# Start offsets of the on-chip pools in a one-layer encoder kernel: all left-hand pools moved to multiples of 512 bytes

## The chip, the cores and the metric

The kernel runs on one core of a Trainium2 chip. The metric is the device time of one launch in microseconds. Before the change three runs gave a median of 2282.25 us (2280.88 to 2286.59).

## The reference, cut to what matters

One layer on x of 1024 tokens by 1024 channels, float32. `rms` is an RMS norm, `mod` an affine map per channel whose shift, scale and gate come from a condition vector.

```python
h = x + 0.5 * g1 * rms(swiglu(mod1(rms(x)), wg1, wu1, wd1))     # 1024 -> 2816 -> 1024
h = h + g2 * rms(mixer(mod2(rms(h))))
h = h + 0.5 * g3 * rms(swiglu(mod3(rms(h)), wg2, wu2, wd2))
...
def mixer(u):
    qa, ka, va, qd, kd, vd, ga, gd = split(u @ w_in)             # 1024 -> 5120
    ya = stick_breaking_attention(qa, ka, va)                    # 8 heads of 64
    yd = rms(differential_attention(qd, kd, vd))                 # 4 heads, two softmax maps
    return (sigmoid(ga) * (ya @ w_sb) + sigmoid(gd) * (yd @ w_da)) @ w_out
```

## The kernel before, in words

**Matmuls in halves.** Every float32 operand is kept as two tiles, a rounded half H and the rest L, and a product is three matmuls into one PSUM bank: H by H, H by L, L by H. `PE.matmul(out, stationary, moving)` loads the stationary operand (128 columns) into TensorE and then streams the moving one (512 columns for most). The profile writes the moving operand first: `bank<-uH,wsH` streams `uH` past the weights `wsH`. A product is thus a stream of matmuls, each with a weight load of its own that runs beside the matmul ahead of it.

**Stages, in order of time.**
- FFN 1 up (lines 298 to 300): 11 pairs of a gate and an up matrix. Each of the 22 is a 2x2 block product done with seven block products instead of eight (Strassen's scheme in Winograd's form), each of 12 matmuls: A11 B11 and A12 B21 (`start_parts`; the moving tiles are `uH`/`uL` of the first half of the tokens, 24 matmuls), then p6, p5, p7, p3, p4 with the moving tiles T2, T1, T3, B22, T4 (60 matmuls). The stationary tiles `wsH`/`wsL` come from `wpool`. So 44 matrices over the two FFNs, 84 matmuls each.
- FFN 1 down (583 to 585): stationary `sbH`/`sbL`, moving `tbH`/`tbL`, both in pool `ffb`.
- Mixer (813 to 1087): the jobs QJob, KJob and GateJob stream `u` tiles past `wsH`/`wsL` (line 813 to 817, output `pps`), for the first half of the tokens and for the second; VJob has them the other way round (`vps`, 256 columns). They are handed out a few matmuls at a time between the attention's own work: `qk` (938, 939), the transposes (955, 956), and weights by values (1021, 1066, 1068: moving `tH`/`tL`, stationary `v`).
- Merge (200 to 202): `bps` streams second-half `u` tiles (holding the attention's results) past `wsH`/`wsL`; `ops` streams output weights past the merged tiles `mH`/`mL`. The weights `wo` come from `wpool`, but of those for the second half of the output columns (q = 1) the first two of four come from a pool of the stage itself (tag `wx`).
- FFN 2 up and down as FFN 1.

**Where tiles lie.** Each pool is a run of bytes in every SBUF partition; each tile's size is rounded up to 32 bytes. Left-hand pools stack upwards: `const`, `upool` (first-half `u` tiles), `wpool` (`wsH`, `wsL`, `raw`), `mpool` (small tiles of the norms), and above them one stage's pools after the other (`ffa`, `fft`, `fft2`, `ffb0`, `ffb`, `u1` with the second-half `u` tiles, `mixa` with `q`, `kd`, `kl`, `v`, and `mrg` with `mH`, `mL`, `wx`). Right-hand pools hang from the top: `ypool`, `late`, and during the attention `mixb` (`be`, `f`, `ex`, `tH`, `tL`). A pool's first byte is the end of the one it stands on, so the tiles of `const` set where `upool` and `wpool` begin, and those of `mpool` where all stage pools begin. Matmul operands are slices of whole multiples of 512 bytes into their tiles (128 columns of 4 bytes), so an operand's offset modulo 512 is that of its tile.

The bytes before the change: 1152 that belong to the runtime and built-in constants; then `const`, 512 + 512 + 32 + 32 + 288 + 96 + 32 + 32 and eight tiles of 32, 1792, so that `upool` begins at 2944 = 5 x 512 + 384. `upool` and `wpool` hold multiples of 512. `mpool` has 2048 + 12 x 32 = 2432, which takes the stage pools to 256 modulo 512.

Of the kernel before, what the change touches and what calls it, by code (L numbers as in the profile page):

```python
# [12 lines left out]
F32 = mybir.dt.float32  # L13
F32R = mybir.dt.float32r
BF16 = mybir.dt.bfloat16
# [5 lines left out]
P = 128  # L21
D = 1024
S = 1024
NK = D // P
# [22 lines left out]
def build(ctx, tc, A, out):  # L47
# [3 lines left out]
    const = ctx.enter_context(tc.tile_pool(name="const", bufs=1))  # L51
# [3 lines left out]
    extra = {}  # L55
    mpool = ctx.enter_context(tc.tile_pool(name="mpool", bufs=1))

    ident = const.tile([P, P], F32, name="ident")
    make_identity(nc, ident)
    ones = const.tile([P, P], F32, name="ones")  # L60
    V.memset(ones, 1.0)

    cT = const.tile([P, NK], F32, name="cT")
    SP.dma_start(cT, A["cT"])
    csil = const.tile([P, NK], F32, name="csil")
    ACT.activation(csil, cT, AF.Silu)
    badaT = const.tile([P, 72], F32, name="badaT")
    npreT = const.tile([P, 3 * NK], F32, name="npreT")
    eps = const.tile([P, 1], F32, name="eps")
    V.memset(eps, EPS)  # L70
# [73 lines left out]

    def rstd_of(src, parts=1):

        junk = mpool.tile([P, D], BF16, name="junk", tag="junk", bufs=1)
        ss = mpool.tile([P, 2], F32, name="ss", tag="ss", bufs=4)
        w = D // parts
        for n in range(parts):  # L150
            ACT.activation(junk[:, n * w:(n + 1) * w], src[:, n * w:(n + 1) * w], AF.Square, scale=1.0 / 32.0, accum_out=ss[:, n:n + 1])
        if parts == 2:
            V.tensor_add(ss[:, 0:1], ss[:, 0:1], ss[:, 1:2])
        sq = mpool.tile([P, 1], F32, name="sq", tag="sq", bufs=4)
        ACT.activation(sq, ss[:, 0:1], AF.Sqrt, bias=eps)
        r = mpool.tile([P, 1], F32, name="rs", tag="rs", bufs=4)
        V.reciprocal(r, sq)
        return r
# [7 lines left out]
    def pre_norm(src, eng=V):  # L166

        r = rstd_of(src)
        if eng is ACT:
            ACT.mul(src, src, r)  # L170
        else:
            eng.tensor_scalar_mul(src, src, r)
# [36 lines left out]
    def post_norm_tile(y, g, res, dst, parts=1, tail=False):  # L209

        r = rstd_of(y, parts)
        cuts = [slice(0, HALF), slice(HALF, D)] if tail else [slice(0, D)]
        for c in cuts:
            V.scalar_tensor_tensor(y[:, c], y[:, c], r, g[:, c], ALU.mult, ALU.mult)
        for c in cuts:
            V.tensor_add(y[:, c], y[:, c], res[:, c])
            SP.dma_start(dst[:, c], y[:, c])
# [544 lines left out]
    pending = ffn("wg1", "wu1", "wd1", start0, pending0, steps1, lambda c: 2 if c == 1 else 5 if c < 10 else 0, steps1b, 0, lambda t: A["x"][t * P:(t + 1) * P, :], lambda t: h_dram[0][t])  # L762

    pending = mixer(locals())

    ffn("wg2", "wu2", "wd2", start_half, pending, lambda fp, psum: mod_gate(fp, psum, 2, 0.5), lambda c: 2 if c > 1 else 0, no_steps, 2, lambda t: h_dram[1][t],
# [4 lines left out]
def mixer(e):  # L771
# [14 lines left out]
    with tc.tile_pool(name="mixa", bufs=1, side="left", reuse_waits="tile") as pa, \  # L786
# [200 lines left out]
        def run_av(it, mms):  # L987
            try:
                it.send(mms)
            except StopIteration:  # L990
                pass

        def y_dst(branch, k, rows, j):
            return y_d[branch, j // 2, k // 2, rows, k % 2, (j % 2) * 256:(j % 2 + 1) * 256]
# [65 lines left out]
        def da_out(h, j, it, vt, fill):  # L1060
            pav = psum.tile([P, HALF], F32, name="pav", tag="av", bufs=1)
            o = pav[:, :256]

            def mms(low, kb, w, qs, first, last):
                cs = slice((h % 2) * P, (h % 2 + 1) * P)
                last_pe[0] = PE.matmul(o[:, qs], vt[:, kb, 0, cs], w, start=first, stop=last)
                if not low:
                    PE.matmul(o[:, qs], vt[:, kb, 1, cs], w, start=False, stop=False)

            run_av(it, mms)  # L1070
            ms = mp.tile([P, 256], F32, name="ms", tag="ms", bufs=1)
            y = mp.tile([P, 256], F32, name="yda", tag="y32", bufs=2)
            ACT.activation(ms, o, AF.Square)
            ACT.copy(y, o)
            fill(1)
            pn = psum.tile([P, HALF], F32, name="pn", tag="z", bufs=3)[:, :256]
            PE.matmul(pn, n.ones, ms, start=True, stop=True)

            V.tensor_scalar(ms, pn, 1.0 / P, EPS, ALU.mult, ALU.add)
            ln = mp.tile([P, 256], F32, name="ln", tag="ln", bufs=1)  # L1080
            ACT.activation(ln, ms, AF.Ln, scale=2.0 ** -64)
            ACT.activation(ln, ln, AF.Exp, scale=-0.5, bias=n.lnb)
            V.tensor_mul(ms, ms, ln)
            V.tensor_mul(ms, ms, ln)
            V.tensor_scalar(ms, ms, -0.5, 1.5, ALU.mult, ALU.add)
            V.scalar_tensor_tensor(ln, ln, subs, ms, ALU.mult, ALU.mult)
            V.tensor_mul(y, y, ln)
            SP.dma_start(y_dst(1, h, slice(0, P), j), y)
# [25 lines left out]
        mp = stack.enter_context(tc.tile_pool(name="mixb", bufs=1, side="right", reuse_waits="tile"))  # L1114
# [3 lines left out]
        SP.dma_start(mask_sb, A["mask_sb"])  # L1118
        dist = mp.tile([P, S], F32, name="dist")
        SP.dma_start(dist, A["dist"])  # L1120
        subT = mp.tile([P, 1], F32, name="subT")
        SP.dma_start(subT, A["subT"])
        subs = mp.tile([P, 1], F32, name="subs")
        V.tensor_scalar_mul(subs, subT, 1.0 - LAMBDA_INIT)
# [23 lines left out]
        for u in range(8):  # L1148
            sb = u < 4
            if u == 4:  # L1150

                with tc.issue_after(last_act[0].ins):
                    load = ACT.add_instruction(mybir.InstLoadActFuncSet(
                        name=nc.get_next_instruction_name(), engine=ACT.engine, act_func_set_id=EXP_LN_TABLE))
# [18 lines left out]
            def fill(n):  # L1173
                seen[0] += n * wt[si]
                advance(max(0, min(total, int(total * seen[0] / points)) - done[0]))
# [8 lines left out]
            for si, (par, j) in enumerate(steps):  # L1184
                if carry is not None:
                    next(carry[0])
                if sb:
                    ws = sb_weights(u, par, j, q, k, fill)
                else:
                    ws = da_weights(u - 4, j, q, k, fill)  # L1190
                if carry is not None:
                    carry[1]()
                if si == 0 and u % 2 == 0 and u > 0:
                    vjob = VJob(u // 4, u % 4 // 2)
                    while vjob.step():
                        pass
                it = av(ws[0], ws[1], j, fill)
                if sb:
                    carry = it, lambda par=par, j=j, it=it, u=u, vt=vjob.out, fill=fill: sb_out(u, par, j, it, vt, fill)
                else:  # L1200
                    carry = it, lambda j=j, it=it, u=u, vt=vjob.out, fill=fill: da_out(u - 4, j, it, vt, fill)
# [150 lines left out]
```

## Time and profile before

| what | value |
|---|---|
| three runs, median | 2282.25 us |
| the profiled execution, first to last instruction (span) | 2278.7 us |
| the same, whole | not given apart from its span; the median is 3.55 us over the span |
| TensorE busy | 2189.4 us (96%), 10420 matmuls |
| VectorE, ScalarE, GpSimd busy | 1566.4, 1043.7, 70.0 us |
| mean granted TensorE clock | 0.989 |

In the timeline a row is one matmul: its start in us, how long it took, its engine and line, what it writes, what it streams, what is loaded. A matmul's row lasts about 0.4 us, but the next starts long before it ends, since they are pipelined. So a stream's pace is read from the starts: the time between the starts of two rows, divided by the number of matmuls between them. Below this is called the **gap**. In the groups "x352" is how many there are, and the numbers behind the bar are busy time, mean duration of one, and the engine's idle time ahead of them with what ended it.

### The profile page before, as it was taken

How to read it: one execution, taken by the hardware profiler on the slowest of the kernel's cores; microseconds unless marked ns; L12 is line 12 of the kernel's file. 1: busy time of each engine (PE TensorE's matmuls, PEld its weight loads, DVE VectorE, ACT ScalarE, POOL GpSimd, SP SyncE). 2: the span in 40 equal slices, each digit the busy share in tenths (PEclk: the TensorE clock that was granted, in tenths of full speed). 3: DMA queues.
4: the chain of work that ended last, by engine and by line, in shares of the span. 5: the costliest groups of instructions: out<-in, count | busy, mean ns of one | idle time of the engine just before them, and what ended most of it. 6: DMA issues, size and time to landing. Idle time of an engine off the chain costs nothing.

```text
span 2278.7 us, 28622 instructions
## 1 busy us (share of the span) xinstructions
PE 2189.4 (96%) x10420; PEld 1792.8 (79%) x10420; DVE 1566.4 (69%) x2612; ACT 1043.7 (46%) x1882; POOL 70.0 (3%) x90
## 2 busy tenths in 40 slices
PE   5999999999999999999999999999999999999998
PEld 3787778878887877878888888788888787787786
DVE  6887876567577687576677577655885666755566
ACT  4633323325465555454454455554733232334454
POOL 1000000000000010011001010000000000000000
PEclk9999999999999999999999999999999999999999
DMA  7274874449786111110211122754474553537666
GB/s 305 85 271 169 292 254 170 145 154 316 246 284 216 62 32 45 38 48 30 62 56 63 48 87 75 248 192 130 153 250 171 178 173 128 189 115 260 217 220 219
DMA packets 137678, 364.38 MB, mean 160 GB/s; under 512 B 16705, under 2 KB 20801, under 8 KB 137537
## 3 DMA queue, kind: packets, MB, share of 16 engines
q1 hardware_dynamic: 135904, 356.79, 46.2%
q0 software_dynamic: 1632, 5.77, 0.7%
q8 instruction: 81, 1.33, 0.2%
q14 instruction: 61, 0.49, 0.1%
HBM read 272.32 MB, written 90.18 MB: 159 GB/s over the span
## 4 chain that ended last, share of the span: by engine, by line
PE 66%; DVE 17%; DMA 10%; ACT 5%; issue 2%; SPq 0%; DVEq 0%; ACTq 0%
PE bank L300 9%; PE bank L298 9%; PE bank L299 9%; PE pps L815 4%; PE pps L813 4%; DMA stg<-d_T 4%; PE pps L817 4%; DVE f L1010 2%; PE bankA L585 2%; PE bankA L584 2%; PE bankA L583 2%; DMA wada<-in_wada 2%; PE vps L813 1%; PE vps L817 1%; PE vps L815 1%
## 5 line engine op out<-in xcount | busy, mean ns | idle before, releaser
L813 PE MATMUL pps<-uH,wsH 128*128 128x512 f32 x512 | 209.7, 410 | 0.0
L815 PE MATMUL pps<-uL,wsH 128*128 128x512 f32 x512 | 205.3, 401 | 0.0
L817 PE MATMUL pps<-uH,wsL 128*128 128x512 f32 x512 | 204.6, 400 | 0.0
L226 DVE TENSOR_TENSOR tbL<-stg,tbH 128x512 fp32r<-128x512 f32 x154 | 105.8, 689 | 107.8 <-ACT tbH L225 107.2
L225 ACT CAST tbH<-stg 128x512 fp32r<-128x512 f32 x154 | 95.6, 621 | 156.1 <-DMA stg<-d_T 114.0
L298 PE MATMUL bank<-uH,wsH 128*128 128x512 f32 x352 | 142.1, 406 | 6.2 <-DVE uH L180 2.9
L584 PE MATMUL bankA<-tbL,sbH 128*128 128x512 f32 x352 | 138.5, 393 | 6.1 <-DVE tbL L226 5.9
L299 PE MATMUL bank<-uL,wsH 128*128 128x512 f32 x352 | 140.6, 400 | 1.5 <-POOL uL L181 1.5
L300 PE MATMUL bank<-uH,wsL 128*128 128x512 f32 x352 | 139.5, 397 | 0.0
L583 PE MATMUL bankA<-tbH,sbH 128*128 128x512 f32 x352 | 138.3, 394 | 0.4 <-ACT sbH L225 0.4
L585 PE MATMUL bankA<-tbH,sbL 128*128 128x512 f32 x352 | 138.4, 393 | 0.1
L142 DVE TENSOR_TENSOR wsL<-raw,wsH 128x1024 fp32r<-128x1024 f32 x72 | 88.0, 1222 | 70.4 <-ACT wsH L141 69.0
L226 DVE TENSOR_TENSOR sbL<-stg,sbH 128x512 fp32r<-128x512 f32 (+1 forms) x176 | 108.0, 619 | 33.2 <-ACT sbH L225 32.6
L225 ACT CAST wsH<-s 128x1024 fp32r<-128x1024 f32 x88 | 91.9, 1050 | 70.5 <-DVE s L332 48.7
L225 ACT CAST sbH<-stg 128x512 fp32r<-128x512 f32 (+1 forms) x176 | 98.1, 564 | 55.2 <-DMA stg<-hd_A 40.4
L365 ACT COPY q<-bank 128x512 f32<-128x512 f32 x44 | 25.8, 587 | 212.4 <-PE bank L300 212.4
L817 PEld LDWEIGHTS pps<-uH,wsL 128*128 128x128 f32 x512 | 96.9, 189 | 17.9
L226 DVE TENSOR_TENSOR wsL<-s,wsH 128x1024 fp32r<-128x1024 f32 x88 | 107.2, 1219 | 4.4 <-ACT wsH L225 4.0
L225 ACT CAST wsH<-raw 128x1024 fp32r<-128x1024 f32 (+1 forms) x88 | 73.2, 834 | 78.7 <-PE bank L299 44.8
L813 PEld LDWEIGHTS pps<-uH,wsH 128*128 128x128 f32 x512 | 97.6, 191 | 14.7
L815 PEld LDWEIGHTS pps<-uL,wsH 128*128 128x128 f32 x512 | 97.2, 190 | 14.6
L583 PE MATMUL bankB<-tbH,sbH 128*128 128x512 f32 x264 | 102.9, 390 | 0.1
(247 smaller groups left out, 5953.7 us busy)
## 6 DMA issues: line engine op xcount, KB each, us to landing
wada<-in_wada SPq DMA_DIRECT2D x56, 512.0 KB, 5.2
raw<-in_wg SPq DMA_DIRECT2D x50, 512.0 KB, 6.5
raw<-in_wu SPq DMA_DIRECT2D x50, 512.0 KB, 4.5
raw<-in_wd SPq DMA_DIRECT2D x44, 512.0 KB, 4.5
stg<-hd_A SPq DMA_DIRECT2D x88, 256.0 KB, 4.5
stg<-d_S SPq DMA_DIRECT2D x88, 256.0 KB, 3.6
stg<-d_T SPq DMA_DIRECT2D x88, 256.0 KB, 3.9
d_S<-s SPq DMA_DIRECT2D x40, 512.0 KB, 2.7
```

The source lines that it names most:

```text
L142: eng.tensor_sub(l, raw, h.bitcast(F32))
L225: ACT.copy(h, src)
L226: V.tensor_sub(l, src, h.bitcast(F32))
L298: PE.matmul(ps, H[:, ks], bH, start=first and k == 0, stop=False, skip_group_check=not first)
L299: PE.matmul(ps, H[:, ks], bL, start=False, stop=False, skip_group_check=not first)
L300: PE.matmul(ps, L[:, ks], bH, start=False, stop=k == 3, skip_group_check=not first)
L583: PE.matmul(ps, sH[:, ts], tH, start=first, stop=False, skip_group_check=not check)
L584: PE.matmul(ps, sH[:, ts], tL, start=False, stop=False, skip_group_check=not check)
L585: PE.matmul(ps, sL[:, ts], tH, start=False, stop=last, skip_group_check=not check)
L813: PE.matmul(ps, aH, bH, start=i == 0, stop=False)
L815: PE.matmul(ps, aH, bL, start=False, stop=False)
L817: PE.matmul(ps, aL, bH, start=False, stop=i == n - 1)
```

## The change

Six places change the size or the place of a tile, and no operation. `cT` and `csil` (32 bytes each) become two slices of one tile `cols` of 128 bytes. `badaT` grows from 288 to 352 bytes, `junk` in `mpool` from 2048 to 2176, `ms` in `mixb` from 1024 to 1120, and `subT` in `mixb` from 32 (4 used) to 64; what reads them reads the same columns as before.

```diff
+    cols = const.tile([P, 32], F32, name="cols")
     ident = const.tile([P, P], F32, name="ident")
...
-    cT = const.tile([P, NK], F32, name="cT")
+    cT, csil = cols[:, :NK], cols[:, NK:2 * NK]
     SP.dma_start(cT, A["cT"])
-    csil = const.tile([P, NK], F32, name="csil")
     ACT.activation(csil, cT, AF.Silu)
-    badaT = const.tile([P, 72], F32, name="badaT")
+    badaT = const.tile([P, 88], F32, name="badaT")[:, :72]
...
-        junk = mpool.tile([P, D], BF16, name="junk", tag="junk", bufs=1)
+        junk = mpool.tile([P, D + 64], BF16, name="junk", tag="junk", bufs=1)
...
-            ms = mp.tile([P, 256], F32, name="ms", tag="ms", bufs=1)
+            ms = mp.tile([P, 280], F32, name="ms", tag="ms", bufs=1)[:, :256]
...
-        subT = mp.tile([P, 1], F32, name="subT")
+        subT = mp.tile([P, 16], F32, name="subT")[:, :1]
```

The built programs hold the same instructions in the same order on every engine, with the same semaphore waits; the addresses differ. `const` now holds 128 + 512 + 512 + 352 + 96 + 32 + 32 + 256 = 1920 bytes, so `upool` begins at 3072 = 6 x 512; `mpool` holds 2560 = 5 x 512. `mixb` is 128 bytes larger and begins that much lower. The offsets modulo 512 of the tiles that TensorE reads:

| tiles | pool | before | after |
|---|---|---|---|
| `uH`, `uL`, first half of the tokens | `upool` | 384 | 0 |
| `wsH`, `wsL` | `wpool` | 384 | 0 |
| T1, T2, T3, T4, B22 | `fft`, `fft2` | 256 | 0 |
| `sbH`, `sbL`, `tbH`, `tbL` | `ffb` | 256 | 0 |
| `uH`, `uL`, second half | `u1` | 256 | 0 |
| `q`, `kd`, `kl`, `v` | `mixa` | 256 | 0 |
| `mH`, `mL`, weights of tag `wx` | `mrg` | 256 | 0 |
| `be`, `ex`, `tH`, `tL` | `mixb`, inside it | 352 | 256 |
| `ident`, `ones` | `const` | 128 | 256 |
| `y`, `macc` | `ypool`, `late` | 480 | 480 |

## Prediction

> **What bounds the kernel now.** I read the page first, then busy time by stage, then the timeline of TensorE in the densest places. The page:
>
> ```profile
> span 2278.7 us, 28622 instructions
> ...
> PE 2189.4 (96%) x10420; PEld 1792.8 (79%) x10420; DVE 1566.4 (69%) x2612; ACT 1043.7 (46%) x1882; POOL 70.0 (3%) x90
> ...
> PE 66%; DVE 17%; DMA 10%; ACT 5%; issue 2%; SPq 0%; DVEq 0%; ACTq 0%
> ```
>
> TensorE is busy 96% of the span and holds two thirds of the chain that ended last; no other engine is over 69%. By stage (first column the stretch in us, then its length, then busy us of TensorE, weight loads, VectorE, ScalarE, GpSimd; these are FFN 1 up from 120 us on, FFN 1 down, mixer, merge, FFN 2 up):
>
> ```profile
> 120.00:503.00 383.00, 378.66 (x1631) 302.79 (x1630) 275.58 (x369) 123.63 (x173) 2.31 (x4) 1.00 0.59 206
> 503.00:734.00 231.00, 222.10 (x989) 182.01 (x988) 160.54 (x251) 119.28 (x221) 1.61 (x3) 0.99 0.81 269
> 734.00:1425.00 691.00, 666.75 (x3811) 568.26 (x3810) 483.48 (x1045) 359.09 (x785) 52.46 (x64) 0.99 0.17 54
> 1425.00:1609.00 184.00, 182.49 (x799) 147.01 (x798) 114.87 (x158) 102.14 (x155) 0.00 (x0) 1.00 0.58 190
> 1609.00:2053.00 444.00, 440.25 (x1904) 353.03 (x1902) 306.14 (x429) 168.28 (x245) 2.17 (x4) 1.00 0.49 168
> ```
>
> In FFN up and merge TensorE is idle for 4.3, 1.5 and 3.8 us of 383, 184 and 444, at a granted clock of 1.00. There, whatever changes the gap between two matmuls changes the end. So the question is whether the gap depends on where operands lie. One matrix of FFN 2 up, on TensorE: the 60 matmuls of p6 to p4, then the 24 with `u` of the next matrix, up to its p6:
>
> ```profile
> 1801.79 0.40 PE L298 MATMUL bank<-T2H,wsH 128*128 128x512 f32 x1
> ...
> 1815.78 0.39 PE L298 MATMUL bank<-uH,wsH 128*128 128x512 f32 x1
> ...
> 1817.16 0.39 PE L298 MATMUL bank<-uH,wsH 128*128 128x512 f32 x1
> ...
> 1821.24 0.40 PE L298 MATMUL bank<-T2H,wsH 128*128 128x512 f32 x1
> ```
>
> 60 gaps in 13.99 us are 233.2 ns each. Then 6 in 1.38 us, 230.0, and 18 in 4.08 us, 226.7. Same line, same weights pool, same shape, no idle time noted; what differs is that `u` lies at 384 modulo 512 like the weights, and T2 to T4 at 256, so 128 apart. After a change of kind some six matmuls pass before the gap settles. FFN 1 down has both operands at 256:
>
> ```profile
> 599.66 0.39 PE L585 MATMUL bankB<-tbH,sbL 128*128 128x512 f32 x1
> ...
> 612.35 0.39 PE L584 MATMUL bankB<-tbL,sbH 128*128 128x512 f32 x1
> ```
>
> 56 gaps in 12.69 us: 226.6. So 256 with 256 goes as 384 with 384; the common offset does not matter, the distance does. The merge has the mirror image, with the stationary operand at 256 throughout and the moving one switching pools after 12 matmuls, first `wx` at 256, then `wpool` at 384:
>
> ```profile
> 1499.70 0.39 PE L200 MATMUL ops<-wsH,mH 128*128 128x512 f32 x1
> ...
> 1502.44 0.40 PE L200 MATMUL ops<-wsH,mH 128*128 128x512 f32 x1
> ...
> 1505.23 0.39 PE L200 MATMUL ops<-wsH,mH 128*128 128x512 f32 x1
> ```
>
> 12 in 2.74 us, 228.3, then 12 in 2.79 us, 232.5, within one output tile. And the mixer's first jobs with second-half `u` (256) past weights at 384:
>
> ```profile
> 763.87 0.39 PE L813 MATMUL pps<-uH,wsH 128*128 128x512 f32 x1
> ...
> 774.80 0.40 PE L817 MATMUL pps<-uH,wsL 128*128 128x512 f32 x1
> ```
>
> 47 gaps in 10.93 us: 232.6. Four places, one pattern: operands at the same offset modulo 512 go at 226.7 ns, operands 128 apart at 232.5 to 233.2. I take 232.8, so 6.1 ns or 2.6% for a matmul.
>
> **The change part by part.** The six edits add and remove no operation, no DMA and no wait; the order on each engine stays. All they do is that the pools of the table begin at 0. So each term is a number of matmuls by a change of gap. The groups that count them, by line and shape:
>
> ```profile
> L813 PE MATMUL pps<-uH,wsH 128*128 128x512 f32 x512 | 209.7, 410 | 0.0
> L298 PE MATMUL bank<-uH,wsH 128*128 128x512 f32 x352 | 142.1, 406 | 6.2 <-DVE uH L180 2.9 <-ACT wsH L225 2.4 <-DVE q L371 0.9
> ...
> L813 PE MATMUL vps<-wsH,uH 128*128 128x256 f32 x256 | 73.1, 286 | 0.0
> ...
> L298 PE MATMUL bank<-T1H,wsH 128*128 128x512 f32 x176 | 70.0, 398 | 0.9 <-DVE q L371 0.9
> ...
> L200 PE MATMUL bps<-uH,wsH 128*128 128x512 f32 x128 | 50.8, 397 | 0.8 <-DVE gt L1259 0.8
> L200 PE MATMUL ops<-wsH,mH 128*128 128x512 f32 x128 | 50.6, 395 | 0.7 <-ACT mH L1264 0.7
> ```
>
> The mean durations here do not show the pattern (410 for the mixer, 398 for T1), since a row's end is modelled; only the starts do.
>
> FFN up, both: 44 matrices. A matrix has 60 matmuls that come from 128 apart to 0 (176 per T group is 44 x 4; five groups, three matmuls each), 60 x 6.1 = 366 ns; its 24 with `u` lose the slow first six, 5.46 us - 24 x 226.7 ns = 19 ns. 44 x 0.385 = 16.9 us, all on the path.
>
> Merge: all of `bps`, 3 x 128, and `ops` but for `wx`, 3 x 96 (a quarter of the weights is in `wx`), are 672 x 6.1 ns = 4.1 us.
>
> Mixer: half of the 3 x 512, the second half of the tokens, 768. They come in runs of three to six between other matmuls, so the gap hardly settles. The first six after a switch went at 230.0, so 2.8 ns each, 2.1 us; the ends are 0 and 768 x 6.1 = 4.7. I take 2.0.
>
> FFN down and `qk` have both operands at one offset before and after: 0.
>
> The price of the matmuls of 256 and 128 columns whose distance changes stands in no row. Their groups, of stick-breaking attention:
>
> ```profile
> L956 PE MATMUL trp<-ident,be 128*128 128x128 f32 x160 | 37.0, 278 | 3.4 <-DVE be L1011 2.0 <-ACT ysb L1025 1.2
> L955 PE MATMUL trp<-ident,be 128*128 128x128 f32 x128 | 34.2, 282 | 0.1
> ...
> L1021 PE MATMUL pav<-tH,v 128*128 128x256 f32 x128 | 28.8, 286 | 0.0
> ```
>
> With those of the differential attention and the shorter ones they are: weights by values (`tH` and `tL` with `v`, from 96 to 256 apart; 560), half of the V jobs (384 of the 3 x 256, from 128 to 0), the transposes of `be` and `ex` (from 224 to 0; 432). No row shows a distance of 256. I bound each by the 6.1 ns of the nearest rows, either way: 1376 x 6.1 = 8.4 us if all go one way. Two of the three come together as the FFN tiles do and one does not, and they sit where TensorE also waits for VectorE, so I take 0 and keep 4 either way.
>
> Sum: 16.9 + 4.1 + 2.0 = 23.0 us. What catches some of it is whoever TensorE waits for. In FFN 1 up, and in the mixer (its longest; who waits, for whom, us in total, times, longest):
>
> ```profile
> PE bank L298 <- ACT wsH L225: 2.1, 2, 1.6
> PE bank L298 <- DVE q L371: 0.9, 1, 0.9
> PE bank L300 <- DVE wsL L226: 0.8, 2, 0.4
> ```
>
> ```profile
> PE pav L1021 <- DVE tL L961: 10.6, 7, 3.0
> ```
>
> These waits are few. Where one stands, TensorE comes to it earlier and waits longer, so the gain since the last such point is lost. VectorE is busy 276 of 383 us in that stage, 72%, so it stays ahead elsewhere. I take a tenth off, 2.3 us: 20.7 us. The span goes from 2278.7 to 2258.0; with the 3.55 us by which the median stands over the span, 2261.5 us.
>
> TensorE's two operands are said to come through two independent read ports, so that loading the next weights takes nothing from the matmul that runs (the Trainium skill, "TensorE: Matmul & The Clock Gate", "Step-by-step: what each phase is for"). By that rule alone all matmuls of one shape have one gap wherever they lie, and the sum would be 0; the rows above with 232.5 beside 228.3 in one output tile do not agree. It is the second rival below.
>
> **The rivals.**
> Producers catch it. If weights preparation on ScalarE and VectorE ran just ahead of TensorE, every ns saved would come back as a wait: half gone gives 2282.25 - 11.5 = 2270.7. Against it: 4.3 and 3.8 us of idle time in the two up stages. For it: the chain gives VectorE 17%, so leads are short in places.
>
> Offsets do nothing. The gaps would then belong to the tiles' roles (T against `u`), and the time stays at 2282. Against it: weights from `wpool` at 384 are slow with a partner at 256 as the loaded operand in FFN up and as the streamed one in the merge, and T tiles have no part there. For it: the layout and the stage change together in most rows. The Trainium skill also holds an operand's start address to be a question of legality, and says that its runs timed nothing there ("SBUF — State Buffer", "Operand start alignment"); no price comes from it.
>
> Offset 0 is itself a slow one. Rows show 256 and 384 in common, never 0. If the gap at a common 0 were 232.8, the about 3960 matmuls of 512 columns that now agree (2 x 528 in up, 1848 in down, the mixer's 768, `wx` 96, `qk` 192) would each pay 6.1, and the 4080 that disagree (2640 in up, 672, 768) would gain nothing: 24.2 us slower, 2306.4. It decides at a gap at 0 of (3960 x 226.7 + 4080 x 232.8) / 8040 = 229.8 ns: above, slower than before. Against it: 256 and 384 agree to 0.1 ns, so nothing suggests that a third value differs.
>
> **How the numbers follow.** A measurement of this kernel can tell about 0.3%, 6.8 us, from no change. Forecast 0.81, producers 0.07, offsets do nothing 0.07, offset 0 slow 0.05. The likeliest gives 2261.5. Its own ends: all of 23.0 and 4 us of the unseen, 2255; 4 us the other way and a fifth lost to waits, 2268. Stretched to the first rival: 2255 to 2272, with no more than 2 in 10 outside. Faster is forecast and first rival, 0.88; same 0.07; slower 0.05.
>
> **What would show it.** In the new timeline, 60 matmuls of T2 to T4 in FFN 2 up should take 13.6 us instead of 13.99 and the `u` run should not start slow; the stretch of FFN 2 up should shrink by 8 us, the merge by 4, FFN down by nothing, the mixer by 2 or less. If T2 to T4 still go at 233, the second rival holds; if FFN down gets slower too, the third; if gaps drop to 227 and TensorE's idle time in FFN up grows by several us, the first. A mixer that moves by more than 4 us either way would mean that the unseen pairs were mispriced.

## The result and the profile after

The changed kernel took 2264.16 us (median of four runs, 2263.80 to 2267.90) against 2282.26 us: ratio 0.9928, interval 0.9914 to 0.9943, so 0.7% or 18 us faster. The forecast was 2261.5 us, with a range of 2255 to 2272. The profiled execution's span fell from 2278.7 to 2261.9 us, by 16.8. The page after:

```profile
span 2261.9 us, 28622 instructions
...
PE 2169.0 (96%) x10420; PEld 1792.0 (79%) x10420; DVE 1565.4 (69%) x2612; ACT 1043.2 (46%) x1882; POOL 70.2 (3%) x90
```

TensorE lost 20 us of busy time with the same 10420 matmuls; the other engines' busy time is unchanged to 1 us. Now the places shown before, in the timeline of TensorE after. First a matrix of FFN 2 up, T2 to T4, then `u`, then the next matrix's T2:

```profile
1789.15 0.39 PE L298 MATMUL bank<-T2H,wsH 128*128 128x512 f32 x1
...
1802.75 0.39 PE L298 MATMUL bank<-uH,wsH 128*128 128x512 f32 x1
...
1808.19 0.39 PE L298 MATMUL bank<-T2H,wsH 128*128 128x512 f32 x1
1808.42 0.39 PE L299 MATMUL bank<-T2L,wsH 128*128 128x512 f32 x1
1808.98 0.50 PE L300 MATMUL bank<-T2H,wsL 128*128 128x512 f32 x1 [0.17 <-DVE wsL L226]
```

60 gaps in 13.60 us, 226.7 ns, where it was 233.2; then 24 in 5.44 us, also 226.7, with no slow start. Between the last two rows 0.56 us pass, with TensorE waiting for weights that VectorE has not finished. That wait is not new: between the same two matmuls it was 0.54 us before the change. Then FFN 1 down, the merge and the mixer's first jobs with second-half `u`:

```profile
589.62 0.39 PE L584 MATMUL bankA<-tbL,sbH 128*128 128x512 f32 x1
...
602.32 0.39 PE L583 MATMUL bankB<-tbH,sbH 128*128 128x512 f32 x1
```

```profile
1487.69 0.39 PE L202 MATMUL ops<-wsH,mL 128*128 128x512 f32 x1
...
1497.89 0.39 PE L202 MATMUL ops<-wsH,mL 128*128 128x512 f32 x1
```

```profile
757.56 0.40 PE L813 MATMUL pps<-uH,wsH 128*128 128x512 f32 x1
...
768.24 0.39 PE L817 MATMUL pps<-uH,wsL 128*128 128x512 f32 x1
```

56 gaps in 12.70 us, 226.8, as before; 45 in 10.20, 226.7, in the merge's output products, where before dozens at 228.3 and at 232.5 took turns; 47 in 10.68, 227.2, where it was 232.6.

**Where the time came from.** Both programs issue the same matmuls in the same order, so each gap between two starts has its counterpart. I call a pair of gaps running if both are under 262 ns, and waiting otherwise, and sum the differences:

| stage | running, 512 columns | running, others | waiting | together |
|---|---|---|---|---|
| FFN 1 up | -7.6 | +0.7 | +2.6 | -4.3 |
| FFN 2 up | -7.7 | 0.0 | +1.7 | -6.0 |
| merge | -4.1 | 0.0 | +1.3 | -2.9 |
| mixer | -2.8 | +0.4 | +0.6 | -1.8 |
| FFN down, both | 0.0 | -0.2 | -1.3 | -1.5 |
| sum | -22.2 | +0.9 | +4.9 | -16.4 |

The remaining 0.3 us lie ahead of the first matmul. So TensorE runs 22 us less, and 5 to 6 us of that come back, mostly as waits. The size of that return differs from one execution to the next. The column also holds gaps of some 0.43 us in stretches of a few us at a granted clock of 0.50 (501.8 to 505.0 us in the profile after), and some of these lie elsewhere in each execution. A second profile of the changed kernel has 8.4 us of waiting against the same profile of before. Without the pairs that touch such a stretch, the two give +6.2 and +6.3 us. FFN 2 up from its first to the first matmul of FFN 2 down, before and after:

```profile
1609.49 0.40 PE L298 MATMUL bank<-uH,wsH 128*128 128x512 f32 x1
...
2052.91 0.40 PE L583 MATMUL bankA<-tbH,sbH 128*128 128x512 f32 x1
```

```profile
1598.58 0.39 PE L298 MATMUL bank<-uH,wsH 128*128 128x512 f32 x1
...
2035.94 0.39 PE L583 MATMUL bankA<-tbH,sbH 128*128 128x512 f32 x1
```

443.4 us became 437.4, by 6 and not the 8 that the gaps alone would give. The group of p6 that reads the L half of the weights, before and after, shows one of the waits (idle time ahead of it at the end of the row):

```profile
L300 PE MATMUL bank<-T2H,wsL 128*128 128x512 f32 x176 | 71.3, 405 | 2.0 <-DVE wsL L226 1.0
```

```profile
L300 PE MATMUL bank<-T2H,wsL 128*128 128x512 f32 x176 | 70.7, 402 | 3.3 <-DVE wsL L226 3.3
```

Its idle time grew from 2.0 to 3.3 us. By pairs, 1.7 of the 4.3 us that came back in the two FFN ups stand ahead of p6's matmuls (moving tile T2), 1.6 ahead of those with T4 and 0.9 ahead of those with B22.

### The profile page after: what moved, and what is told of

Read it like the earlier page. It is cut to its first block, busy times and chain, and to the rows that moved or that the text cites. A ratio compares the mean times of both kernels' runs of the same rounds, so it can differ in the third digit from the quotient of the medians.

```text
span 2261.9 us, 28622 instructions
## 1 busy us (share of the span) xinstructions
PE 2169.0 (96%) x10420; PEld 1792.0 (79%) x10420; DVE 1565.4 (69%) x2612; ACT 1043.2 (46%) x1882; POOL 70.2 (3%) x90
```

## The experiments

The theory: the distance between the streamed and the loaded operand modulo 512 sets the gap. Rivals: an operand has to begin at a multiple of 512; the tiles' roles set the gap. Gaps below are means of those under 250 ns, by the starts in the trace, and the rows quoted are the ends of 60 gaps T2 to `u` unless it is said otherwise. Ratios are to the kernel before on the same chip.

**Only the norms' scratch tile padded.** On the kernel before:

```diff
-        junk = mpool.tile([P, D], BF16, name="junk", tag="junk", bufs=1)
+        junk = mpool.tile([P, D + 64], BF16, name="junk", tag="junk", bufs=1)
```

> Only the norms' scratch tile is padded by 128 bytes, so the stage pools move from 256 to 384 modulo 512, where the weights and the first-half u tiles have always been; nothing begins at a multiple of 512. Theory (the distance between the streamed and the loaded operand decides): all products of 512 columns have distance 0, gap 227 ns in FFN up and merge, time 2264 to 2267. Rival (an operand must begin at a multiple of 512): nothing gained, gaps stay at 232 to 233, 2282.

```profile
1837.85 0.39 PE L298 MATMUL bank<-T2H,wsH 128*128 128x512 f32 x1
...
1851.45 0.39 PE L298 MATMUL bank<-uH,wsH 128*128 128x512 f32 x1
```

13.60 us: 226.7 ns. Ratio 0.9932 (0.9914 to 0.9951), median 2267.89 us. One of the six edits gives the same ratio as all six, with both operands of every product of 512 columns at 384 and none at a multiple of 512. By pairs the running gaps of these products lose 22.4 us here, against 22.2 for the six. The profiled execution was the slowest of the four (2273.0 us), with 13 us more of waiting than before. The rival of alignment falls.

**Only the constants' pool changed.** The change without the pads of `junk`, `ms` and `subT`.

> Only the constants' pool is changed, so weights and first-half u tiles lie at 0 and the stage pools at 384, again 128 apart. Theory (distance): gap of T1 to T4 and of the merge stays at 232 to 233, time 2280 to 2284. Rival (multiples of 512): one of the two operands is aligned, so a part of the gain, some 2272, with gaps between 227 and 233.

```profile
1839.93 0.40 PE L298 MATMUL bank<-T2H,wsH 128*128 128x512 f32 x1
...
1853.92 0.39 PE L298 MATMUL bank<-uH,wsH 128*128 128x512 f32 x1
```

13.99 us: 233.2, as before. Ratio 0.9999 (0.9986 to 1.0013). Weights at a multiple of 512 bring nothing while their partners lie 128 off.

**256 apart.** On the kernel before, `D + 192` in place of `D + 64`: weights at 384, stage pools at 128.

> The norms' scratch tile is padded by 384 bytes: weights and first-half u tiles at 384, stage pools at 128, so 256 apart. If the pattern repeats every 512 bytes, 256 is as far as it goes: gap 232 to 233 or more, 2280 to 2284 or slower. If it repeats every 256 bytes, 256 is as good as 0: gap 227, 2264 to 2267.

```profile
1867.38 0.39 PE L298 MATMUL bank<-T2H,wsH 128*128 128x512 f32 x1
...
1880.98 0.39 PE L298 MATMUL bank<-uH,wsH 128*128 128x512 f32 x1
```

13.60 us: 226.7. Ratio 0.9927 (0.9911 to 0.9943). So 512 is not the period: 256 apart is as good as 0. The change aligned twice as far as it needed to.

**FFN down put apart.** On the kernel after, an unused tile of 128 bytes ahead of the streamed tiles of FFN down:

```diff
-                            s, t = halves(fp, raw(sn, c), "sb", SB), halves(fp, raw(tn, c), "tb", NPAIR)
+                            s = halves(fp, raw(sn, c), "sb", SB)
+                            if p == 0 and c == 0:
+                                fp.tile([P, 32], F32, name="pad", tag="pad", bufs=1)
+                            t = halves(fp, raw(tn, c), "tb", NPAIR)
```

> The kernel after, with an unused tile of 128 bytes between the loaded and the streamed tiles of FFN down, so that these are 128 apart where all kernels so far had 0. Theory (distance): the 1848 products of FFN down go from 227 to 232.8 ns, 11 us slower than after if nothing absorbs it, so 2272 to 2276. Rival (FFN down is fast for another reason, its own pools or its order): 2264, gaps stay at 227.

The first and the last row of 56 gaps of FFN 1 down:

```profile
598.65 0.40 PE L583 MATMUL bankB<-tbH,sbH 128*128 128x512 f32 x1
...
611.66 0.40 PE L585 MATMUL bankB<-tbH,sbL 128*128 128x512 f32 x1
```

13.01 us: 232.3, where after had 226.8. This stage, which the change had left as it was, takes on the slow gap as soon as its operands are put 128 apart; so it is not the tiles' roles. Paired with the kernel after, the running gaps of the two FFN downs grew by 11.0 us, the amount expected, while waiting gaps there shrank by 5. Of these 1.5 us are gaps at half the granted clock that this execution did not have in that place; that in the rest TensorE comes later to what it used to wait for is argued, not shown. Ratio 0.9958 (0.9941 to 0.9975), median 2273.98 us. The kernel after was not timed beside it; by the ratios this is 5 to 7 us over it (0.9928 and, in a second series, 0.9935), and the intervals overlap a little. So it is the gaps that show the effect, and the whole time only agrees.

**64, 32 and 96 apart.** On the kernel before, `D + 96`, `D + 80` and `D + 112`. One run each.

> The norms' scratch tile is padded by 192 bytes: stage pools 64 above the weights. 0 and 256 apart gave 227 ns, 128 apart 232.9. If every distance that is no multiple of 256 costs the same, 232 to 233 in FFN up and 2280 or so. If the cost grows with the distance from a multiple of 256, some 230 and 2273. If the pattern repeats every 64 bytes, 227 and 2265.

> Padded by 160 bytes: 32 apart, the smallest step that the pools allow. Every distance but multiples of 256 costs: 232 to 233, 2280. Cost in proportion: 228.5, 2269. Repeats every 32 bytes: 227, but then 128 apart could not have been slow, so this is out.

> Padded by 224 bytes: 96 apart. Every distance but multiples of 256 costs: 232 to 233, 2280. Cost in proportion: 231.5, 2277. If 64 is the period, 96 goes as 32.

The T2 to `u` runs of 64, 32 and 96, in this order:

```profile
1832.34 0.40 PE L298 MATMUL bank<-T2H,wsH 128*128 128x512 f32 x1
...
1846.09 0.40 PE L298 MATMUL bank<-uH,wsH 128*128 128x512 f32 x1
```

```profile
1848.20 0.40 PE L298 MATMUL bank<-T2H,wsH 128*128 128x512 f32 x1
...
1862.21 0.40 PE L298 MATMUL bank<-uH,wsH 128*128 128x512 f32 x1
```

```profile
1847.20 0.40 PE L298 MATMUL bank<-T2H,wsH 128*128 128x512 f32 x1
...
1861.21 0.40 PE L298 MATMUL bank<-uH,wsH 128*128 128x512 f32 x1
```

13.75 us, 229.2; 14.01 us, 233.5; 14.01 us, 233.5. Times 2271.58, 2289.11 and 2287.88 us beside 2284.02 for the kernel before. So the cost is not in proportion to the distance: 32 off costs as much as 96 or 128. The times of 32 and 96 stand 8 to 9 us over the 2280 expected; paired with the kernel before, the products of 512 columns account for 2 to 3 us more, and the rest is waiting, of one execution each. 64 stands alone. It is half-way in FFN up; in the merge's products `bps`, where the streamed operand lies 64 above the loaded one as in FFN up, the mean is 231.2; in the merge's output products, where the distance is 64 the other way, the mean of 282 gaps is 233.4. Neither of the simple rules fits 64.

**S2 prepared first.** The waits in FFN up stand ahead of p6, for the halves of S2. On the kernel after, the two casts and two subtractions of S2 and S1 are done in pieces:

```diff
-            H, L = halves(wpool, s21.rearrange("p a b -> p (a b)"), "ws", 4, D)
+            H = wpool.tile([P, D], F32R, name="wsH", tag="wsH", bufs=4)
+            L = wpool.tile([P, D], F32R, name="wsL", tag="wsL", bufs=4)
+            for i in range(2):
+                c = slice(i * HALF, (i + 1) * HALF)
+                ACT.copy(H[:, c], s21[:, i])
+                V.tensor_sub(L[:, c], s21[:, i], H[:, c].bitcast(F32))
```

> The kernel after, with the preparation of S2 and S1 in FFN up cut in two pieces of 512 columns, so that S2, which p6 reads first, is ready about 0.9 us earlier and S1 about as before; two more instructions on ScalarE and on VectorE for each of 44 matrices. Theory (what the change lost in FFN up went to p6 waiting for S2's halves): the stalls ahead of T2, about 10 us in all after the change, go for the most part, 5 to 8 us faster than after, 2256 to 2259. Rival (the preparation starts late for another reason, its transfer or VectorE's queue): under 2 us, 2262 to 2265, or slower by the added work.

Ratio 0.9902 (0.9885 to 0.9918), median 2261.36 us, 2.8 under the kernel after and in neither of the two ranges expected. Since that interval meets the changed kernel's from another chip, both were run once more on one chip, along with a third kernel:

> The kernel after once more, on the chip and beside the kernel before that the next two are timed on: ratio 0.992 to 0.9935 to the kernel before.

> The kernel after with S2 prepared first, on the same chip as the kernel after. Theory (a part of what the change gained in FFN up went to p6 waiting for S2): 2 to 6 us faster than the kernel after, ratio to before 0.989 to 0.9915. Rival (the two medians so far came from different chips and differ by that): same ratio as the kernel after to within 0.001.

The kernel after: 0.9935 (0.9923 to 0.9947), 2267.33 us. S2 first: 0.9910 (0.9897 to 0.9922), 2261.81 us. The intervals do not overlap; 5.5 us by the medians. The group of p6 with S2 first:

```profile
L300 PE MATMUL bank<-T2H,wsL 128*128 128x512 f32 x176 | 68.8, 391 | 0.0
```

The 3.3 us of idle time, which the second profile of the kernel after has too, are gone. A part of the waiting moved on to the `u` of the next matrix, in the kernel after and with S2 first:

```profile
L298 PE MATMUL bank<-uH,wsH 128*128 128x512 f32 x352 | 143.0, 409 | 6.2 <-DVE uH L180 2.7 <-ACT wsH L225 2.6 <-DVE q L371 0.8
```

```profile
L298 PE MATMUL bank<-uH,wsH 128*128 128x512 f32 x352 | 143.4, 410 | 9.3 <-ACT wsH L225 4.2 <-DVE uH L180 2.7 <-DVE q L376 2.3
```

The two FFN ups take 472.7 and 434.9 us, against 476.3 and 436.8 for the kernel after on the same chip: 5.5 us, as much as the whole gain. That is more than the 1.7 us by which the waits ahead of p6 had grown with the change, so most of what this edit takes away was there before the change. It shows what these waits cost, and not that they alone took back what the change gave. Of all kernels here this is the fastest.

**Without the pads in the attention's pool.** On the kernel after, `ms` and `subT` as before.

> The kernel after without the two pads in the attention's own pool: tH and tL go back to 352 modulo 512 beside v at 0, so 96 from a multiple of 256 where after they are at a multiple of 256; be and ex go to 96 beside ident. Theory (these matmuls of 256 and 128 columns pay little): mixer stage as after to within 2 us, same time. Rival (they pay the same 6 ns as the long ones, 560 and 432 matmuls): up to 6 us slower than after.

Ratio 0.9926 (0.9913 to 0.9939), median 2264.69 us; the mixer takes 688.2 us against 688.9 and 689.2 in the two profiles of the kernel after. These two pads do nothing that can be measured in the time.

## Why the prediction was right, and where it was off

**The gap.** Forecast: 232.8 ns fall to 226.7. Measured: 226.7 to 227.2 in all four places. The distance as the cause is shown by undoing it on one side (only constants: 0.9999), making it in another way (only the scratch tile: 0.9932) and putting it where it had not been (FFN down: 11 us more of running time).

**The terms.** FFN up, 16.9 forecast, 15.3 in running gaps; merge 4.1 and 4.1; mixer 2.0 and 2.8; FFN down 0 and 0. Sum 23.0 and 22.2. The FFN term was high because the prediction took 226.7, the settled gap of one matrix, for all: the gaps under 250 ns of the T matmuls had a mean of 232.8 before, as forecast, and of 227.1 after, so 5.7 and not 6.1.

**The waits.** This is the step that was mis-sized: "I take a tenth off, 2.3 us". The waiting gaps took 4.9 us and other running gaps 0.9, a quarter of the 22.2; by the second profile it was 8.4, some 2 us of them at half the clock, and 1.2, a third without those 2. The forecast leaned on VectorE's busy share of 72%, and the chain's 17% for VectorE was the warning. Why a share of 72% does not keep VectorE ahead is argued, not shown: p6 asks for S2 at a fixed point, and what is late there is one string of transfer, sum, cast and subtraction. The idle time in the group of p6 was 2.0 us before and 3.3 after. Preparing S2 first gave 5.5 us, but most of that wait was there before the change. The prediction has p6's wait among its rows, as one of a few, and names no place where waits would grow; they grew at p6, T4, B22 and in the merge (1.3 us).

**From span to time.** I carried 3.55 us over from a median. In every run of the kernel after the time stands 1.8 to 2.0 us over the span, and in 31 further runs of the kernel before 1.8 to 2.1. So the profiled execution of before took some 2280.6 us and was a shorter one than the median, by an estimate from these differences. That accounts for the span having fallen by 16.8 and the median by 18.1. With 1.9 in place of 3.55 the forecast would have been 2259.9, 4.3 us off and not 2.7: that part was luck.

**The unseen pairs** of 256 and 128 columns: taken at 0 with 4 us either way. Of those, the transposes and the weights by values were tried by themselves and came to 0 within the interval. The V jobs were not, but the traces show them, and they go the other way. 94 gaps of the first V job with second-half `u` (`vps`, streaming 256 columns of `wsH` and `wsL`), before and after:

```profile
775.03 0.28 PE L813 MATMUL vps<-wsH,uH 128*128 128x256 f32 x1
...
786.18 0.28 PE L815 MATMUL vps<-wsL,uH 128*128 128x256 f32 x1
```

```profile
768.47 0.28 PE L813 MATMUL vps<-wsH,uH 128*128 128x256 f32 x1
...
779.74 0.28 PE L815 MATMUL vps<-wsL,uH 128*128 128x256 f32 x1
```

11.15 us are 118.6 ns each, 128 apart; 11.27 us are 119.9, at one offset. With only the constants' pool changed, again 128 apart, it is 118.6, and 256 apart 119.9. So at 256 columns one common offset costs 1.3 ns, 0.5 us for the 384 matmuls, about the mixer's +0.4 of other running gaps. The bound of 6.1 ns held, but the sign that the long products show did not carry over.

**The rivals.** Offset 0 is not slow. Roles do not matter. By the Trainium skill's statement that loading the next weights takes no read bandwidth from the running matmul ("TensorE: Matmul & The Clock Gate", "Step-by-step: what each phase is for") one would expect no change; the ratio of 0.9928 disagrees with that expectation. What the two reads share is not shown by any run here: theory and experiments speak of distances only. Producers that catch the gain were the rival nearest to what happened, with a quarter to a third instead of a half.

**What the theory had wrong** is its modulus: 256 apart goes as 0 apart, so it is 256 bytes and not 512, and 64 fits no simple rule. That did not change the forecast, since all the pools went to one offset.

## What to carry to other kernels

Where TensorE is the bound, read its pace from the starts of consecutive matmuls, and compare stretches of one shape: here 2.6% lay between two layouts that the mean durations and the waits of the one profile did not show. Where products are like these, of 512 columns, give the streamed and the loaded tile the same offset modulo 256 bytes; here one pad in the right pool was enough, and a change of the small tiles in front of the operands can undo it. For the products of 256 columns here it gained nothing. When the bound engine is made faster, look for the point where it asks for something at a fixed place in the program, and have that piece made first.

## What the runs showed of the hardware that was not expected

Products of 512 columns in this kernel ran at 226.7 to 227.2 ns at distances of 0 and 256 bytes, and at 232.3 to 233.5 at 32, 96 and 128. At 64 they ran at 229.2 (FFN up) and 231.2 (`bps` of the merge) with the streamed operand above the loaded one, and at 233.4 with it below, which stays unexplained. The V jobs, of 256 columns, had the opposite order: 119.9 to 120.0 ns per matmul at distances of 0 and 256, 118.6 at 128, 117.3 at 96, 118.3 at 32 and 113.6 to 117.8 at 64. After a switch from distance 128 to 0 the first six gaps were 230.0 ns on the average before 226.7 was reached. In the mixer, where products come mostly in runs of two to eight between other shapes, the mean of the gaps under 250 ns was 230.0 (231.8 before) even with all operands of those products at one offset.
